# Pricing the other engine's work: a planning model that charges VectorE and GpSimd for steps that overlap

## The chip, the cores and the metric

The kernel runs on one core of one Trainium2 chip. A core has engines that each work through their own queue of instructions in order and wait for each other by semaphores: TensorE (PE, matrix products; PEld is its loading of weights), VectorE (DVE), ScalarE (ACT), GpSimd (POOL) and SyncE (SP), whose queue starts most of the DMAs. What counts is the device time of one execution in microseconds (us): the median of several runs, lower being better. A profiled execution gives a trace; its span is the time from its first to its last instruction.

## What is computed

One layer of a hybrid decoder trunk on 16 learned and 1024 given tokens of 1024 channels. Four token mixers (RWKV-7, gated linear attention, attention over keys selected by an indexer, mLSTM) read one combined input projection; their outputs are gated, summed and projected; then 16 SwiGLU experts follow, of which each token uses two. Cut to the frame:

```python
h = layer_norm(concat(meta, x), ln_in_g, ln_in_b)
p, gates = split(h @ w_in)                  # 1040 tokens; 4 branches, and 4 * 1024 gate channels
y = [rwkv7(p[0]), gla(p[1]), dsa(p[2]), mlstm(p[3])]          # 256 channels each
m = sum(sigmoid(gates[i]) * (y[i] @ w_branch[i]) for i in range(4))
h = layer_norm(alpha * h + m @ w_out, ln1_g, ln1_b)
out = layer_norm(alpha * h + hier_moe(h), ln2_g, ln2_b)       # top group, then top 2 of its 4 experts
```

## The kernel before

Every large product is taken in three passes of a rounded format: a matrix is split into a high part (a cast by ScalarE) and a low part, raw minus high, a subtraction of two operands. The subtractions carry names in the trace: hTl for the normalised input, wl for w_in, fwl for w_branch, yl and zl for the mixers' outputs, wol for w_out, mT0l and s9l for weights of the experts.

**Stages.** In the head (0 to 58 us) `InputNorm` (L368) normalises nine tiles of tokens, lx; VectorE adds, GpSimd multiplies, PE transposes (lp), and ScalarE and VectorE split into hTh and hTl. Then `Products` (L605) runs through w_in in tiles of 128 columns, 2 groups of 24 matmuls into pj each, 148 groups in all. Beside them the mixers run as streams: `rwkv` builds an inverse by forward substitution on GpSimd (ft and TT by turns, about 283 to 355 us) and then goes through a recurrence (xp, xc); `dsa` scores keys at the same time (xa and xb are products, rl the rectified result on ScalarE, sc the weighted sum over heads on VectorE), selects and attends; `gla` and `mlstm` follow. `Merge` (L443) multiplies each branch's output (yh, yl; zh, zl) by w_branch into mz, in rows of two halves of six matmuls, 32 rows in all. A row's gate comes from PE directly (fused) or is read back from memory into g; VectorE makes g times mz, and GpSimd or VectorE adds it to the sum h. From 1217 us on w_out, the second normalisation, the routing, and the experts.

**What sets the order.** Nothing in this order is written out by hand. While the program is built, the class `Order` (L30) keeps a clock for each of four engines, `t`, and moves it with every instruction: `before` (L93) finds when the operands are there, `after` (L133) adds the modelled cost of the step. Streams that are ready by PE's clock go first; where PE would wait, `fill` (L60) draws the next piece of projection work. Three places ask the other clocks too. `free` (L197) gives a step to GpSimd if its clock is behind PE's, else to VectorE (every wl); `sooner` (L201) gives it to whichever would be done first (fwl, yl, zl); and the sums h go to GpSimd unless its clock is 0.6 us ahead of PE's (L600). `more` (L2817) draws pieces of w_out while VectorE's clock is behind PE's. The prices before are a fixed part and a part by size:

```python
return 0.068 + n / 960 + (0.061 if op == "scalar_tensor_tensor" and len(ins) > 2 else 0)    # VectorE, us
...
... 0.14 + n * (0.0044 if op == "tensor_scalar" else 0.0021)                                 # GpSimd, us
...
return self.gpsimd if self.t["gpsimd"] < self.t["tensor"] else self.vector                  # free
```

So what the model holds for an engine's time decides which of two engines gets a step, and in what order the streams' steps and the filling work stand in each queue. Once built, the order is fixed.

Of the kernel before, what the change touches and what calls it, by code (L numbers as in the profile page):

```python
# [15 lines left out]
PSUM = bass.MemoryType.PSUM  # L16
# [13 lines left out]
class Order:  # L30
# [10 lines left out]
    def __init__(self, nc):  # L41
        self.nc = nc
        self.t = {e: 0.0 for e in ("tensor", "vector", "scalar", "gpsimd")}
        self.ready = {}

        self.wrote, self.used = {}, {}

        self.last, self.rings, self.prior = {}, {}, {}
        self.table = 1
        self.tiling = 128, 128  # L50
        self.end = 0.0
        self.dma = 0.0
        self.back, self.in_back = None, False

        self.warm = None
        for e in self.t:
            setattr(self, e, Engine(self, e))
        self.sync = Engine(self, "sync")
# [74 lines left out]
    def after(self, eng, op, kw, out, ins, dep):  # L133
        n = out.free_size()
        if "dma" in op:
            start = max(dep, self.t["tensor"])
            if eng == "gpsimd":
                start = self.t[eng] = max(self.t[eng], dep) + 1.03
            end = max(start + 0.6, self.dma) + n * out.shape[0] * 4 / 340e3
            if start < self.t["tensor"] + 1:  # L140
                self.dma = end
            end += 1.8
        else:
            self.acc = kw.get("accum_out") is not None
            end = self.t[eng] = max(self.t[eng], dep) + getattr(self, "cost_" + eng)(op, out, ins, n)
            end += self.OUT[eng]
            if eng != "tensor":
                for a in [out] + ins:
                    self.note(self.used.setdefault((eng, a.tensor.name), []), a, end)
# [5 lines left out]
        if kw.get("accum_out") is not None:  # L155
            a = kw["accum_out"]
            self.note(self.wrote.setdefault(a.tensor.name, []), a, end)
            self.ready[a.tensor.name] = end
        self.end = end


    TURN = 0.092
# [442 lines left out]
class Products:  # L605
# [127 lines left out]
    def run(self, ln, done, es):  # L733
# [21 lines left out]
        yield from self.gated(self.last, self.after)  # L755

    def gated(self, i, after):

        m, q, nc = self.merge, [], self.k.nc
# [45 lines left out]
        while m.G is None:  # L805
            yield False
            ahead()
        self.flush()
        more = after()
        while True:  # L810
            ahead()
# [2276 lines left out]
```

## Time and profile before

| | us |
|---|---|
| median of three runs | 1682.43 |
| lowest and highest | 1677.73, 1683.59 |
| the profiled execution | 1686.26 |
| its span | 1684.5 |
| PE busy in the span | 1587.0 |
| VectorE, ScalarE, GpSimd busy | 1114.9, 755.7, 431.0 |
| mean granted clock of PE | 0.971 of full speed |

The profiled execution is 3.83 us above the median, and 1.76 of it lie outside the span. Almost all instructions are recorded by one helper, so they bear its line, L268, and are told apart by the names of the tiles that they write and read. A busy engine is one that works on an instruction; waits are idle time before an instruction, with what ended it.

### The profile page before, as it was taken

To read this page: it belongs to the slowest core of one execution; us is meant where nothing else is said; L and a number is where in the kernel's file an instruction comes from. 1 tells how busy PE (TensorE), PEld (TensorE's weight loads), DVE (VectorE), ACT (ScalarE), POOL (GpSimd) and SP (SyncE) were. 2 spreads that over 40 slices of the span, in tenths; PEclk is the share of its full clock that TensorE was granted. 3 is DMA by queue.
4 is the path that set the end of the run, shared out by engine and by line. 5 is a ranking of instruction groups with operands and counts; after the bars stand their busy time and mean duration, and the time that the engine had idled before them with its cause. 6 is when DMAs were issued, how large, how long until landed. Compare 5 with 4: busy or idle time off the path is not lost. (4 is left out here: it accounts for less than half of the span.)

```text
span 1684.5 us, 27808 instructions
## 1 busy us (share of the span) xinstructions
PE 1587.0 (94%) x10020; PEld 1336.2 (79%) x10020; DVE 1114.9 (66%) x2534; ACT 755.7 (45%) x1544; POOL 431.0 (26%) x555
## 2 busy tenths in 40 slices
PE   4999999899999999999999999997999989999985
PEld 3999899788887777777887777775788778898962
DVE  8344755754489898884556477748666668776655
ACT  4334444355544455425444433432121157776645
POOL 5222226831111102123211131126800123111021
PEclk9999999999999999999999998998999989999997
DMA  7874445242322323343211252067512379999855
GB/s 245 240 231 133 146 132 146 80 124 78 91 67 78 83 79 104 95 154 108 69 38 32 86 152 63 28 193 251 180 66 101 126 213 265 287 303 279 269 196 201
DMA packets 240429, 244.86 MB, mean 145 GB/s; under 512 B 39018, under 2 KB 204812, under 8 KB 240288
## 3 DMA queue, kind: packets, MB, share of 16 engines
q1 hardware_dynamic: 234400, 222.08, 43.8%
q0 software_dynamic: 5888, 20.97, 4.4%
q8 instruction: 80, 1.31, 0.3%
q14 instruction: 61, 0.50, 0.1%
HBM read 168.98 MB, written 74.02 MB: 144 GB/s over the span
## 5 line engine op out<-in xcount | busy, mean ns | idle before, releaser
L268 PE MATMUL pj<-hTl,wh 128*128 128x512 f32 (+3 forms) x1184 | 435.5, 368 | 1.0 <-DVE hTl L268 1.0
L268 PE MATMUL pj<-hTh,wh 128*128 128x512 f32 (+3 forms) x1184 | 435.2, 368 | 0.0
L268 PE MATMUL pj<-hTh,wl 128*128 128x512 f32 (+3 forms) x1184 | 431.5, 364 | 0.0
L268 PEld LDWEIGHTS pj<-hTh,wh 128*128 128x128 f32 (+1 forms) x1184 | 225.8, 191 | 26.8 <-issue 2.5
L268 PEld LDWEIGHTS pj<-hTl,wh 128*128 128x128 f32 (+1 forms) x1184 | 225.6, 191 | 26.5 <-issue 1.6
L268 POOL TENSOR_TENSOR wl<-wr,wh 128x256 fp32r<-128x256 f32 (+1 forms) x177 | 137.8, 795 | 422.9 <-ACT wh L268 407.0
L268 PEld LDWEIGHTS pj<-hTh,wl 128*128 128x128 f32 (+1 forms) x1184 | 226.0, 191 | 23.7 <-issue 1.6
L268 ACT COPY pe<-pj 128x384 f32<-128x384 f32 (+3 forms) x84 | 37.4, 445 | 121.9 <-PE pj L268 83.7
L268 DVE SCALAR_TENSOR_TENSOR sc<-rl,wi,sc 128x512 f32<-128x512 f32 (+3 forms) x77 | 58.7, 762 | 42.4 <-ACT rl L268 39.3
L268 ACT CAST wh<-wr 128x256 fp32r<-128x256 f32 (+1 forms) x240 | 85.1, 402 | 1.0 <-DMA wr<-in_w_in_dram 0.9
L268 ACT ACTIVATE pe<-pj 128x512 f32<-128x512 f32 x64 | 38.1, 595 | 100.4 <-PE pj L268 74.8
L268 POOL TENSOR_TENSOR h<-h,g 128x512 f32<-128x512 f32 x46 | 64.7, 1420 | 51.9 <-issue 32.2
L268 POOL DMA_INDIRECT xg<-h1d,ix x32 | 33.7, 1054 | 155.4 <-PE py L268 148.7
L268 ACT ACT_TABLE_LOAD x47 | 60.3, 1283 | 6.3 <-DVE qk L268 2.6
L268 PE MATMUL pg<-xT,mT0h 128*128 128x384 f32 x208 | 62.4, 362 | 0.0
L268 POOL TENSOR_TENSOR sc<-sc,band 128x256 f32<-128x256 f32 (+1 forms) x32 | 24.4, 764 | 124.1 <-DVE sc L268 84.8
L268 PE MATMUL pg<-xT,mT0l 128*128 128x192 f32 x208 | 53.8, 259 | 0.0
L268 DVE TENSOR_TENSOR mT0l<-raw,mT0h 128x1024 fp32r<-128x1024 f32 x35 | 42.5, 1219 | 14.5 <-ACT mT0h L268 13.0
L268 ACT COPY PT<-xb 128x512 f32<-128x512 f32 (+3 forms) x56 | 27.4, 490 | 54.9 <-PE xb L268 52.7
L268 PEld LDWEIGHTS po<-v,PT 128*128 128x128 f32 x352 | 46.3, 192 | 5.6 <-ACT PT L268 2.5
L268 DVE TENSOR_TENSOR wl<-wr,wh 128x256 fp32r<-128x256 f32 x63 | 39.9, 653 | 12.9 <-ACT wh L268 12.8
L268 PE MATMUL po<-v,PT 128*128 128x64 f32 x352 | 47.6, 273 | 0.5 <-ACT PT L268 0.4
(645 smaller groups left out, 3769.5 us busy)
## 6 DMA issues: line engine op xcount, KB each, us to landing
wr<-in_w_in_dram SPq DMA_DIRECT2D x59, 512.0 KB
raw<-in_moe_w_gate_dram SPq DMA_DIRECT2D x32, 512.0 KB
raw<-in_moe_w_up_dram SPq DMA_DIRECT2D x32, 512.0 KB
raw<-in_moe_w_down_dram SPq DMA_DIRECT2D x32, 512.0 KB
gtd<-pe SPq DMA_DIRECT2D x52, 256.0 KB
g<-gtd SPq DMA_DIRECT2D x52, 256.0 KB
ys<-ey SPq DMA_DIRECT2D x14, 768.0 KB
ys<-zero SPq DMA_DIRECT2D x8, 960.0 KB
```

Source lines behind the costliest of these rows:

```text
L268: r = f(*args, **kw)
```

## The change

`Order` keeps, for VectorE and for GpSimd, the modelled intervals of their last twelve steps that read two operands of more than 16 elements a row outside PSUM. When such a step is added on one of the two, its price rises by a share of the time for which it overlaps the other engine's intervals: 0.8 of it on VectorE, 0.3 on GpSimd. The clocks that all choices read move with it.

```diff
--- before.py
+++ after.py
@@ -41,6 +41,8 @@
     def __init__(self, nc):
         self.nc = nc
         self.t = {e: 0.0 for e in ("tensor", "vector", "scalar", "gpsimd")}
+        self.two = {"vector": [], "gpsimd": []}
         self.ready = {}
 
         self.wrote, self.used = {}, {}
@@ -142,7 +144,11 @@
             end += 1.8
         else:
             self.acc = kw.get("accum_out") is not None
-            end = self.t[eng] = max(self.t[eng], dep) + getattr(self, "cost_" + eng)(op, out, ins, n)
+            start = max(self.t[eng], dep)
+            c = getattr(self, "cost_" + eng)(op, out, ins, n)
+            if eng in self.two and self.pair(op, ins):
+                c = self.beside(eng, start, c)
+            end = self.t[eng] = start + c
             end += self.OUT[eng]
             if eng != "tensor":
                 for a in [out] + ins:
@@ -157,6 +163,22 @@
             self.note(self.wrote.setdefault(a.tensor.name, []), a, end)
             self.ready[a.tensor.name] = end
         self.end = end
+
+    SHARED = dict(vector=0.8, gpsimd=0.3)
+    def pair(self, op, ins):
+        return sum(a.space != PSUM and a.free_size() > 16 for a in ins) > 1
+    def beside(self, eng, start, c):
+        other = self.two["gpsimd" if eng == "vector" else "vector"]
+        c += self.SHARED[eng] * sum(max(0.0, min(start + c, b) - max(start, a)) for a, b in other)
+        mine = self.two[eng]
+        mine.append((start, start + c))
+        del mine[:-12]
+        return c
     TURN = 0.092
```

No line that computes is different. The built program has the same 8788 instructions on PE and 1524 on ScalarE; VectorE has 2358 in place of 2364, GpSimd 609 in place of 603. Of the 240 wl GpSimd has 181 in place of 177; yl goes from 2 to 4 on GpSimd, zl and s9l from none to 1, fwl from 4 to 3; VectorE adds g to h three times in place of two. Seven of the 32 rows have fused gates in place of six, so that gate results of 256 KB are written and read back 50 times and not 52.

Three places. First VectorE's queue in the head (lx, hTl and wl as above; bst and mv are batch statistics); before:

```order
16 L268 TENSOR_TENSOR lx_121<-lx_121,gb 128x1024
17 L268 TENSOR_TENSOR lx_123<-lx_123,gb 128x1024
18 L268 TENSOR_TENSOR lx_121<-lx_121,gb 128x1024
19 L268 TENSOR_TENSOR wl<-wr,wh 128x256 x2
20 L268 TENSOR_TENSOR lx_123<-lx_123,gb 128x1024
21 L268 TENSOR_TENSOR wl<-wr,wh 128x256 x2
22 L268 BN_STATS bst_166<-lx_129 128x6
23 L268 TENSOR_TENSOR hTl<-lp,hTh 128x4x128 x2
```

and after:

```order
16 L290 TENSOR_TENSOR lx_121<-lx_121,gb 128x1024
17 L290 TENSOR_TENSOR lx_123<-lx_123,gb 128x1024
18 L290 TENSOR_TENSOR lx_121<-lx_121,gb 128x1024
19 L290 TENSOR_TENSOR wl<-wr,wh 128x256 x4
20 L290 BN_STATS bst_166<-lx_129 128x6
21 L290 TENSOR_TENSOR lx_123<-lx_123,gb 128x1024
22 L290 TENSOR_TENSOR hTl<-lp,hTh 128x4x128
23 L290 BN_STATS bst_166<-lx_129 128x6
```

Four wl stand together now ahead of the next tile's lx addition, and the batch statistics are further ahead.

Next GpSimd's queue towards the end of the forward substitution (ft and TT, which shrink by a column at each step), which ends before ARz is cleared for the recurrence; before:

```order
143 L268 TENSOR_TENSOR TT<-TT,ft 104x33x7
144 L268 TENSOR_TENSOR ft<-Ms,TT 104x204
145 L268 TENSOR_TENSOR TT<-TT,ft 104x34x6
146 L268 TENSOR_TENSOR wl<-wr,wh 128x256
147 L268 TENSOR_TENSOR ft<-Ms,TT 104x175
148 L268 TENSOR_TENSOR TT<-TT,ft 104x35x5
```

and after, some steps earlier:

```order
127 L290 AFFINE_SELECT sc<-sc 128x128
128 L290 TENSOR_TENSOR ft<-Ms,TT 104x351
129 L290 TENSOR_TENSOR TT<-TT,ft 104x27x13
130 L290 TENSOR_TENSOR wl<-wr,wh 128x256
131 L290 TENSOR_TENSOR ft<-Ms,TT 104x336
```

The wl of the first listing is gone from the last fifteen steps; one stands earlier, after the step of 351 columns.

Last VectorE's queue where the merge stretch's first w_out pieces are split; before:

```order
1326 L268 TENSOR_TENSOR wol<-raw,woh 128x1024 x3
1327 L268 TENSOR_TENSOR yl<-fr,yh 128x2x256
1328 L268 SCALAR_TENSOR_TENSOR g<-g,mz 128x512 x2
1329 L268 TENSOR_TENSOR fwl<-fw,fwh 128x256
1330 L268 SCALAR_TENSOR_TENSOR g<-g,mz 128x512 x2
1331 L268 TENSOR_TENSOR fwl<-fw,fwh 128x256
1332 L268 SCALAR_TENSOR_TENSOR g<-g,mz 128x512
1333 L268 TENSOR_TENSOR yl<-fr,yh 128x2x256
1334 L268 SCALAR_TENSOR_TENSOR g<-g,mz 128x512
```

and after:

```order
1325 L290 TENSOR_TENSOR wol<-raw,woh 128x1024 x3
1326 L290 TENSOR_TENSOR yl<-fr,yh 128x2x256
1327 L290 SCALAR_TENSOR_TENSOR g<-g,mz 128x512 x2
1328 L290 TENSOR_TENSOR fwl<-fw,fwh 128x256 x3
1329 L290 TENSOR_TENSOR yl<-fr,yh 128x2x256
1330 L290 TENSOR_TENSOR wol<-raw,woh 128x1024
1331 L290 TENSOR_TENSOR fwl<-fw,fwh 128x256
1332 L290 TENSOR_TENSOR yl<-fr,yh 128x2x256
1333 L290 SCALAR_TENSOR_TENSOR g<-g,mz 128x512
1334 L290 TENSOR_TENSOR h_9861<-h_9861,g 128x512
1335 L290 SCALAR_TENSOR_TENSOR g<-g,mz 128x512
1336 L290 TENSOR_TENSOR zl<-fr,zh 128x2x256
```

The block of three wol is the same; behind it the next fwl, wol and yl stand ahead of the following g, and zl, which came after the seventh wol before, comes between.

## Rows read from the trace of the kernel before

**Rows 1.** The page: its span, and busy time of each engine with share and instructions.

```profile
span 1684.5 us, 27808 instructions
PE 1587.0 (94%) x10020; PEld 1336.2 (79%) x10020; DVE 1114.9 (66%) x2534; ACT 755.7 (45%) x1544; POOL 431.0 (26%) x555
```

**Rows 2.** Stages: length; busy us of PE, PEld, DVE, ACT, POOL; PE clock; DMA; GB/s.

```profile
0.00:58.00 58.00, 33.36 (x188) 29.95 (x189) 46.31 (x83) 29.06 (x55) 27.15 (x27) 0.94 0.68 226
...
283.00:361.00 78.00, 70.03 (x396) 65.14 (x395) 51.80 (x59) 35.68 (x79) 61.20 (x71) 0.93 0.38 103
361.00:612.00 251.00, 250.11 (x2224) 207.47 (x2222) 176.49 (x526) 123.50 (x294) 39.32 (x64) 1.00 0.30 81
612.00:1099.00 487.00, 482.37 (x2744) 382.34 (x2742) 335.45 (x883) 206.55 (x441) 102.08 (x160) 0.98 0.29 85
1099.00:1217.00 118.00, 102.14 (x416) 79.73 (x414) 77.62 (x103) 26.16 (x50) 66.66 (x55) 0.96 0.69 218
1217.00:1400.00 183.00, 173.69 (x1026) 149.93 (x1025) 123.18 (x356) 56.83 (x96) 24.16 (x29) 0.95 0.42 134
```

**Rows 3.** What PE waited for in 0:58: us, times, longest.

```profile
PE lp L268 <- DVE lx L268: 20.7, 4, 16.6
```

**Rows 4.** What PE waited for in 283:361.

```profile
PE xb L268 <- ACT rl L268: 3.6, 3, 1.2
PE xp L268 <- POOL ARz L268: 2.5, 1, 2.5
PE xa L268 <- ACT rl L268: 1.8, 3, 1.2
```

**Rows 5.** What PE waited for in 361:1099, the largest.

```profile
PE x L268 <- DVE e L268: 1.8, 1, 1.8
```

**Rows 6.** What PE waited for in 1099:1217.

```profile
PE mz L268 <- DVE fwl L268: 6.6, 5, 1.9
PE mz L268 <- DVE g L268: 6.4, 5, 1.5
PE mz L268 <- POOL fwl L268: 2.9, 1, 2.9
```

**Rows 7.** DVE in order of time, the additions on lx: start, length, idle before.

```profile
32.30 3.41 DVE L268 TENSOR_TENSOR lx<-lx,gb 128x1024 f32<-128x1024 f32 x1
...
36.83 2.20 DVE L268 TENSOR_TENSOR lx<-lx,gb 128x1024 f32<-128x1024 f32 x1
...
44.11 1.21 DVE L268 TENSOR_TENSOR lx<-lx,gb 128x1024 f32<-128x1024 f32 x1
...
53.28 1.22 DVE L268 TENSOR_TENSOR lx<-lx,gb 128x1024 f32<-128x1024 f32 x1
```

**Rows 8.** POOL in the same stretch.

```profile
29.87 11.38 POOL L268 TENSOR_TENSOR lx<-lx,gb 128x1024 f32<-128x1024 f32 x4 [4.62 <-ACT lx L268]
```

**Rows 9.** DVE in 283:361 by form, min/median/max ns: subtractions wl and score steps.

```profile
L268 DVE TENSOR_TENSOR wl<-wr,wh x14: 572/1106/1261, 292.0 to 347.1; 128x256 fp32r<-128x256 f32 x14
...
L268 DVE SCALAR_TENSOR_TENSOR sc<-rl,wi,sc x35: 351/850/1452, 291.2 to 351.6; 128x512 f32<-128x512 f32 x21, 128x128 f32<-128x128 f32 x7, 128x256 f32<-128x256 f32 x7
```

**Rows 10.** The same score steps on DVE in 361:612.

```profile
L268 DVE SCALAR_TENSOR_TENSOR sc<-rl,wi,sc x28: 606/751/753, 364.3 to 436.3; 128x512 f32<-128x512 f32 x21, 128x384 f32<-128x384 f32 x7
```

**Rows 11.** DVE, the subtractions wol of the whole run.

```profile
L268 DVE TENSOR_TENSOR wol<-raw,woh x8: 1221/2294/2316, 1133.1 to 1172.4; 128x1024 fp32r<-128x1024 f32 x8
```

**Rows 12.** Two stretches with a low PE clock, same columns as rows 2.

```profile
318.50:325.30 6.80, 5.63 (x20) 5.03 (x19) 6.17 (x8) 2.04 (x7) 5.56 (x6) 0.51 0.37 108
356.00:359.40 3.40, 3.40 (x18) 3.38 (x18) 0.00 (x0) 2.61 (x6) 1.31 (x2) 0.53 0.47 112
```

**Rows 13.** PE in order of time: first of twelve mz, and of two following pj groups.

```profile
1106.11 0.39 PE L268 MATMUL mz<-yh,fwh 128*128 128x512 f32 x1
...
1108.89 0.39 PE L268 MATMUL pj<-hTh,wh 128*128 128x512 f32 x1
...
1114.43 0.40 PE L268 MATMUL pj<-hTh,wh 128*128 128x512 f32 x1
```

## The prediction

> **What bounds the kernel now.** I read the page's busy shares first: TensorE (PE) works 1587.0 of 1684.5 us, VectorE (DVE) 66%, GpSimd (POOL) 26% [rows 1]. So the time is PE's own work plus what PE loses, about 97 us, and a change that only moves instructions can win or lose only there. The busy time by stage says where the loss lies [rows 2]: of 0:58 PE is idle 24.6 us, of 283:361 8.0, of 1099:1217 15.9, of 1217:1400 9.3; between 361 and 1099, 738 us of it, only 5.5. Then I asked in those stages what PE waited for. In the head it is lx, the normalised input, four times [rows 3]. In 283:361 it is rl and ARz: rl is an output of ScalarE whose buffers VectorE frees by summing scores, ARz is GpSimd's to clear, behind the forward substitution [rows 4]. In 361:1099 the longest wait is 1.8 us [rows 5]. In 1099:1217, where the last gated products are summed, it is fwl and g, on VectorE but for one fwl on GpSimd, 15.9 us together [rows 6]. These are the stages where VectorE and GpSimd work side by side.
>
> They do disturb each other. In the head three equal 128x1024 additions on VectorE took 3.41, 2.20 and 1.21 us [rows 7]; the slow ones lie under GpSimd's four products, 11.38 us without a gap [rows 8]. Among the scores a 128x256 wl subtraction has a median of 1.11 us and a fastest of 0.57, and a score step goes up to 1.45 [rows 9]; after GpSimd's long run the slowest of the same steps is 0.75 [rows 10]. Of eight wol subtractions the fastest took 1.22 us and the median 2.29 [rows 11].
>
> **What the change does.** No arithmetic and no wait is written differently. The model's price of a two-operand step rises by 0.8 (VectorE) or 0.3 (GpSimd) of its overlap with such steps on the other engine, so on VectorE by at most 0.8 of its own length. By the model's formula a wl subtraction of 0.335 us may become 0.60, a wol one of 1.135 may become 2.04; the rows have 1.11 and 2.29. The sign is right and wol's size nearly, wl's is half. What follows is only a new order: some subtractions change engine (GpSimd gets four more wl of 177, two yl, one zl, one s9l; VectorE one fwl, one h), and PE's streams are handed out at other places. What moves costs the same few microseconds of engines that are not the bound; it counts only where PE waits. By stages:
>
> Head (0:58). VectorE does four wl before the third tile's lx addition where it did two, so that addition comes two wl later, 2 x 0.5 = about 1 us, and what PE does behind it about 2.5 us later with the hTl steps that slipped too. This is not lost for good: PE then waits for lx anyhow. Replaying VectorE's queue in its new order with the durations of these rows, the batch statistics of later tiles come earlier, and the last tile's addition is issued at 51.6 us in place of 53.28 [rows 7], with seven more small products of PE done before it. The first matmuls' delay is inside the 16.6 us wait that ends the longest of the four [rows 3]. I take 1.3 us of gain from the 1.7; the bounds are 0.8 lost (2.5 late, 1.7 regained) and 1.7 won.
>
> Scores beside the substitution (283:361). Three wl stood on GpSimd in front of ARz, now one, and the order gives PE 67.2 groups of 24 projection matmuls before the recurrence's first product in place of 65.9. The first of 24 starts at 1108.89 and the next group's at 1114.43, so a group of 512 columns is 5.54 us [rows 13] and 1.3 of the narrower ones of this stage some 6.5. Against the 2.5 us wait for ARz [rows 4] that is ample: it goes, and with it the stretch at 356.0:359.4 in which the granted clock was 0.53, that is 1.2 GHz, right behind that wait [rows 12]: half of 3.4 us, 1.7. Of the rl waits, 5.4 us together [rows 4], the five long ones are of about 1.2; with one wl less among the score steps of 306 to 320 at 1.11 us [rows 9] and another now and then moved, I take 1.7 off. Together 5.9. From below: if both clock and rl stay, 2.5; from above all of 5.4 + 2.5 + 1.7 and the half of 318.5:325.3 (3.4) [rows 12], 13.
>
> Recurrence to the last stream (361:1099). Between the recurrence's first and last product PE has 26.8 groups in place of 29.2, so 2.4 x 5.54 = 13.3 us less to do while it waits for that chain; from the selection of keys to the end of the last mixer 1.5 groups and two halves of 6 matmuls less, 11 us (twelve mz matmuls go from 1106.11 to 1108.89, so a half is 1.39) [rows 13]. The work is not lost, it stands later. It costs only where the cover was thin. PE was idle 0.9 us of 251 in 361:612 and 4.6 of 487 after it [rows 2], so the trace does not show how much of the cover was spare. Bounds: 0, and the whole 13.3. I take 1.0, near the low end: no wait of this stage is above 1.8 [rows 5], and 2.4 of 29.2 groups is a twelfth of the cover.
>
> The merge stretch (1099:1217). From 1108.89 PE had two groups and 27 rows of two halves, 11.1 + 27 x 2.78 = 86 us, and took until 1217: 22 lost, of which the waits are 15.9 [rows 6] and the clock some 4.7 (0.96 of 118) [rows 2]. After the change the last stream ends about 19 us of PE's work sooner, so that six groups instead of three and 29 rows remain, and three pairs of groups stand between rows: there the staging of y and z and three wol run beside projections instead of beside rows that each need a g and an fwl. But 22 rows still follow the last pair, the three wol still stand in one block before the first g, and each row still asks VectorE for two g, one fwl and the h that GpSimd does beside it. Counting the waits of the new order by hand with these durations gives the same 16 us within what I can tell. I take 0, with 5 either way.
>
> Experts and end (1217 on). The order is the same but for one s9l, at 1400 us, that goes from VectorE (1.22 us as the fastest wol of the same shape [rows 11]) to GpSimd, where a gather queues behind it; 0, with 1 either way.
>
> The sum is -1.3 - 5.9 + 1.0 + 0 + 0 = -6.2, on the profiled execution's 1686.26 us: 1680.1. That execution was 3.83 above the median of 1682.43, so I say 1676.5 for the median.
>
> The Trainium skill, on its page "SBUF — State Buffer", section "Who interferes with whom", says that a VectorE step with two inputs in SBUF and a GpSimd step that reads SBUF hold the port they share in turn, each for its whole length, and that the one that comes second stands still. The 3.41 us beside 1.21 agrees: 2.2 us more is most of a GpSimd product of 2.85 (11.38 / 4) and more than the 0.8 x 1.21 = 0.97 that the change would charge. By that rule each of the eight subtractions that the new order moves to GpSimd (four wl, two yl, one zl, one s9l) stands once in the way of a VectorE step, at 1.11 - 0.57 = 0.54 us each [rows 9]; were all of it on the path, the sum would be -6.2 + 4.3 = -1.9 by the rule.
>
> **The rivals.** *The merge stretch opens* (against: 22 rows in a line at the end). If the three pairs of groups take up the wol block and the staging, only the tail's waits stay. Half of the 15.9 us and one clock dip of 3.4 us at half speed (1.7) would go: 9.6 more, about 1667.
>
> *The recurrence runs bare* (slower). Its steps are a chain PE, VectorE, ScalarE, PE; with 13.3 us less between its ends PE would stand whenever a step's own chain is longer than the work put between. It decides from the point where the spare of the cover, not seen in the trace, is under 13.3 us. If none of it was spare: +13.3, and one dip as at 318.5:325.3 (half of 6.8 us, 3.4) [rows 12]: 1676.5 - 1.0 + 16.7 = about 1692. For it: 0.9 us of idle time says the old cover was just used up or more. Against: no wait there is even 1 us.
>
> *The order hardly matters* (it doesn't do what it says). The charge meets at most half of what a wl loses, few subtractions change engine, and the waits of the merge and score stages come back beside other work. Then only the ARz wait goes, or is paid for elsewhere: 1680 to 1685, say 1682. The rule of the Trainium skill's page "SBUF — State Buffer", section "Who interferes with whom", speaks for this rival: if the later step stands still for the rest of the other engine's, a charge by the share of its own length misses the price.
>
> **How the numbers follow.** Forecast 1676.5: 0.40. The merge stretch opens, 1667: 0.20. The order hardly matters, 1682: 0.25. The recurrence runs bare, 1692: 0.15. About 0.5% (8.4 us) is what a measurement of this kernel can tell from no change, so faster means under 1674.0 and slower over 1690.8. Faster: most of the merge rival and two fifths of the forecast, whose own spread is some 6 us: 0.18 + 0.16 = 0.34. Slower: 0.10 of the recurrence rival and a few hundredths of the others: 0.13. Same: 0.53. The range reaches from a merge stretch that opens by more than half (1664) to a recurrence with almost no spare (1691).
>
> **What would show it.** Right: no wait for ARz before the recurrence, and no low clock behind it; waits for rl near 3.7 us; PE idle 361:1099 near 6.5 us; in the merge stretch fwl and g again near 16 us; the last lx some 1.7 us sooner. Wrong: PE waiting for the recurrence's steps (xc, xp) or the last mixer's by more than 5 us, or a merge stretch whose waits halve or double, or a clock below 0.97 over the span.

## The result: the changed order is slower by about 10 us

| | before | changed |
|---|---|---|
| median of eight runs, us | 1679.1 | 1688.81 |
| lowest and highest, us | 1675.39, 1683.59 | 1686.5, 1695.72 |
| the profiled execution, its span, us | 1686.26, 1684.5 | 1690.72, 1688.9 |
| mean granted clock of PE | 0.971 | 0.972 |

The ratio is 1.0064, 95% interval 1.0045 to 1.0082: slower by 9.7 us, by more than the 0.5% of the prediction. The forecast was 1676.5, a gain; the time lies in the range (1664 to 1691), on the other side of no change. The changed kernel measured again later gave 1.0065 (1.0043 to 1.0087).

The two profiled spans differ by 4.4 us and not by 9.7: the execution profiled before lay 7.2 us above its median of eight runs, that of after 1.9. So single stages are compared below with further traces of either order too.

First the busy times on the page of the changed kernel, as [rows 1]:

```profile
PE 1580.8 (94%) x10020; PEld 1331.6 (79%) x10020; DVE 1118.9 (66%) x2528; ACT 755.6 (45%) x1544; POOL 436.1 (26%) x561
```

PE is idle 108.1 us, where it was 97.5. The stages, with the columns of [rows 2]:

```profile
0.00:58.00 58.00, 31.82 (x187) 29.11 (x188) 48.64 (x82) 28.40 (x54) 28.41 (x27) 0.97 0.71 234
283.00:361.00 78.00, 69.37 (x400) 64.31 (x399) 48.26 (x58) 34.25 (x79) 59.76 (x69) 0.97 0.34 90
361.00:612.00 251.00, 246.41 (x2195) 204.96 (x2194) 179.85 (x534) 124.83 (x296) 35.86 (x60) 0.99 0.31 82
612.00:1099.00 487.00, 480.22 (x2767) 381.49 (x2766) 338.82 (x879) 207.51 (x443) 105.25 (x165) 1.00 0.32 93
1099.00:1217.00 118.00, 102.68 (x422) 80.73 (x421) 72.52 (x95) 26.32 (x51) 72.38 (x60) 0.92 0.59 180
```

Length minus PE's busy time gives the idle time. In 283:361 it is 8.6 us, where it was 8.0: in the score stage, from which the forecast took most of its gain, no idle time went, and only the clock is somewhat better, 0.97 for 0.93. From 361 to 1099 it is 4.6 + 6.8 = 11.4, where it was 5.5. The merge stretch has 15.3 for 15.9. What PE waited for at the recurrence's start, 283:375 (us, times, longest), to be held against [rows 4]:

```profile
PE xa L290 <- ACT rl L290: 4.9, 6, 1.3
PE xp L290 <- ACT UV L290: 2.3, 1, 2.3
PE xp L290 <- issue: 1.5, 1, 1.5
PE pj L290 <- ACT pe L290: 1.3, 1, 1.3
PE xb L290 <- ACT rl L290: 0.2, 1, 0.2
```

The wait for ARz is gone, as forecast. In its place stand three waits of 5.1 us together, for steps of ScalarE (the one put down to "issue" too, below). How long each of the three is differs from trace to trace (in e1, the same kernel again, 0.9 + 2.5 + 2.2). And the waits for rl are 5.1 us for 5.4, not 3.7.

**Where they come from.** SyncE's queue before, from 339 us, in order of time (start, length of the start):

```profile
339.03 0.34 SPq L268 DMA_DIRECT2D pD<-pe  x1
...
342.92 0.34 SPq L268 DMA_DIRECT2D pD<-pe  x1
348.19 0.32 SPq L268 DMA_DIRECT2D td<-TT  x1
```

and after:

```profile
329.52 0.32 SPq L290 DMA_DIRECT2D pD<-pe  x1
346.31 0.34 SPq L290 DMA_DIRECT2D td<-TT  x1
346.70 0.58 SPq L290 DMA_DIRECT2D BKg<-bkd  x1
347.38 2.06 SPq L290 DMA_DIRECT2D pD<-pe  x1
...
355.59 0.54 SPq L290 DMA_DIRECT2D pD<-pe  x1
...
357.73 0.40 SPq L290 DMA_DIRECT2D pD<-pe  x1
```

pe is the copy that ScalarE takes of a finished projection group; it has three buffers, and a buffer is free when its store to memory (pD) has landed. td is the store of the substitution's result TT, ready at 346.3. Before, td stood behind the pe stores. Now it stands ahead of three of them, and SyncE starts nothing from 329.84 to 346.31. ScalarE behind it (idle time and what ended it in brackets):

```profile
353.09 0.48 ACT L290 COPY pe<-pj 128x384 f32<-128x384 f32 x1 [4.29 <-DMA pD<-pe]
...
357.69 0.39 ACT L290 COPY pe<-pj 128x272 f32<-128x272 f32 x1 [3.19 <-DMA pD<-pe]
358.10 0.58 ACT L290 COPY UV<-xp 40x512 f32<-40x512 f32 x1
...
361.66 1.04 ACT L290 CAST qs<-qi 128x1024 fp32r<-128x1024 f32 x1 [2.55 <-DMA qi<-pC]
362.73 0.69 ACT L290 ACTIVATE KB<-xp,half 104x512 f32<-104x512 f32 x1
```

The stores leave at 347.38 and, behind loads that need td's landing, at 355.59, so the copies wait until 353.09 and 357.69, and UV, the recurrence's first step on ScalarE, stands behind the second. KB stands behind qs, whose input is one more load of the same queue; PE's product xp starts at 363.51, when KB's 0.69 us are over, so its "issue" is KB. The granted clock in the window right behind the wait for UV (it ended at 358.73) and at two later places (columns of [rows 2]):

```profile
359.20:362.60 3.40, 2.79 (x10) 2.28 (x8) 0.00 (x0) 0.94 (x1) 1.17 (x2) 0.50 1.01 257
458.20:461.60 3.40, 3.19 (x29) 2.63 (x30) 3.00 (x12) 1.67 (x4) 0.00 (x0) 0.50 0.00 1
1403.70:1410.50 6.80, 5.55 (x13) 3.77 (x14) 6.18 (x27) 2.63 (x4) 0.00 (x0) 0.50 0.41 122
```

0.50 is 1.2 GHz. A wait of 1.6 to 2.3 us (at the third place two, of 2.2 and 1.9) is followed there by 3.4 us at half the clock, at the third place by 6.8, and half of PE's busy time in it is lost on top of the wait.

The second place, 458.2, is in the recurrence. VectorE, before and then changed:

```profile
466.95 1.20 DVE L268 TENSOR_SCALAR_CACHE_REDUCE junka<-sc 128x1024 bf16<-128x1024 f32 x1
```

```profile
456.80 1.21 DVE L290 TENSOR_SCALAR_CACHE_REDUCE junka<-sc 128x1024 bf16<-128x1024 f32 x1
...
457.94 0.41 DVE L290 TENSOR_SCALAR UV<-xc 40x256 f32<-40x256 f32 x1
```

UV, a step of the recurrence, stands behind the counting steps of the key selection (junka), which reach VectorE 10 us earlier in the recurrence than before. PE's wait for it, 1.6 us, is in every trace with the changed order at this place (also e1, e3, e5, e10, e13 and e17), whatever SyncE's queue does there; the old order has 0.5. PE's waits of 361:1099, as [rows 5]:

```profile
PE xp L290 <- issue: 1.7, 2, 1.5
PE xc L290 <- DVE UV L290: 1.6, 1, 1.6
PE x L290 <- DVE hall L290: 1.5, 3, 0.6
PE po L290 <- ACT PT L290: 1.5, 1, 1.5
PE x L290 <- DVE e L290: 1.2, 1, 1.2
PE pj L290 <- ACT pe L290: 1.2, 1, 1.2
```

No long wait, but five of 1.2 to 1.6 us. In the merge stretch, as [rows 6]:

```profile
PE mz L290 <- DVE g L290: 10.8, 5, 6.0
PE mz L290 <- POOL fwl L290: 2.9, 1, 2.9
```

Five waits for VectorE's fwl have gone, and one of 6.0 us for g has come: behind the block of wol, as long as what it replaces.

**The experts.** One instruction moved there, s9l. VectorE and then GpSimd at 1396 us:

```profile
1396.80 2.37 DVE L290 TENSOR_SCALAR fs<-sf 128x16 f32<-128x16 f32 x1
```

```profile
1396.15 2.98 POOL L290 TENSOR_TENSOR s9l<-raw,s9h 128x1024 fp32r<-128x1024 f32 x1 [1.52 <-ACT s9h L290]
```

fs took 0.16 us before. In the changed kernel with s9l alone back on VectorE:

```profile
1399.91 0.17 DVE L290 TENSOR_SCALAR fs<-sf 128x16 f32<-128x16 f32 x1
```

So one subtraction given to GpSimd cost a step of VectorE 2.2 us, and that step reads one operand, of 16 elements: the change, which charges steps with two operands of more than 16, prices it at nothing. The Trainium skill, page "SBUF — State Buffer", section "Who interferes with whom", says that a `tensor_scalar` can take the shared port pair as well, and that the later of the two stands still; these two rows agree: fs starts 0.65 us after s9l and ends with it, at 1399.17 and 1399.13.

### The profile page after: what moved, and what is told of

Same layout as the page of the kernel before. It is cut to its first block, busy times and chain, and to the rows that moved or that the text cites. A ratio compares the mean times of both kernels' runs of the same rounds, so it can differ in the third digit from the quotient of the medians.

```text
span 1688.9 us, 27785 instructions
## 1 busy us (share of the span) xinstructions
PE 1580.8 (94%) x10020; PEld 1331.6 (79%) x10020; DVE 1118.9 (66%) x2528; ACT 755.6 (45%) x1544; POOL 436.1 (26%) x561
## 5 line engine op out<-in xcount | busy, mean ns | idle before, releaser
L290 POOL TENSOR_TENSOR wl<-wr,wh 128x256 fp32r<-128x256 f32 (+1 forms) x181 | 141.9, 800 | 437.1 <-ACT wh L290 418.8
L290 ACT CAST wh<-wr 128x256 fp32r<-128x256 f32 (+1 forms) x240 | 85.8, 402 | 1.1 <-DMA wr<-in_w_in_dram 1.0
L290 ACT CAST mT0h<-raw 128x1024 fp32r<-128x1024 f32 x36 | 37.6, 1051 | 23.2 <-DMA raw<-in_moe_w_up_dram 10.1
```

The costliest lines, as they stand in the source:

```text
L290: r = f(*args, **kw)
```

## Experiments

All were timed in five rounds beside the kernel before on the same chip. The stages meant by "charge only where" are cut by the model's own clock of PE (`self.t["tensor"]`), which runs behind the real one; outside the cut the price is the old one. The order behind a cut still shifts somewhat, since the plan goes on from where the cut left it.

To compare traces beyond one profile's luck, PE's whole loss was added up in each: its idle time, and half of the time in which it worked at the lower clock, up to the last product. The first column is how long SyncE stood for TT (its wait list, 283:370).

| kernel | SyncE for TT, us | PE idle + clock loss, us | ratio (95%) |
|---|---|---|---|
| before | 4.8 | 87.6 + 39.3 = 126.9 | 1 |
| e18 before, td by GpSimd | 4.9 | 89.5 + 32.2 = 121.7 | 1.0011 (0.9990 to 1.0032) |
| e2 charge in the head | 4.9 | 92.7 + 26.4 = 119.1 | 0.9970 (0.9953 to 0.9986) |
| e4 charge behind the recurrence | 5.2 | 85.8 + 28.8 = 114.6 | 0.9983 (0.9962 to 1.0005) |
| e11 charge in the tail | 4.8 | 91.4 + 29.0 = 120.4 | 1.0013 (0.9997 to 1.0030) |
| e8 charge in all but the scores | 4.8 | 89.1 + 28.2 = 117.3 | 0.9996 (0.9976 to 1.0016) |
| e14 e8 with s9l back | 4.8 | 88.1 + 21.6 = 109.7 | 0.9982 (0.9962 to 1.0002) |
| e15 double charge | 4.1 | 87.1 + 25.7 = 112.8 | 0.9937 (0.9916 to 0.9959) |
| changed | 16.4 | 98.3 + 34.5 = 132.8 | 1.0064 (1.0045 to 1.0082) |
| e1 changed again | 17.5 | 97.0 + 35.9 = 132.9 | 1.0065 (1.0043 to 1.0087) |
| e13 changed, s9l back | 17.5 | 98.8 + 33.5 = 132.3 | 1.0058 (1.0037 to 1.0078) |
| e17 changed, td by GpSimd | 17.5 | 100.1 + 32.9 = 133.0 | 1.0066 (1.0043 to 1.0089) |
| e3 charge in the scores | 16.3 | 99.5 + 25.0 = 124.5 | 1.0041 (1.0020 to 1.0061) |
| e7 charge on GpSimd alone | 14.6 | 91.9 + 34.2 = 126.1 | 1.0025 (1.0007 to 1.0042) |
| e12 charge on VectorE alone | 16.5 | 99.3 + 29.0 = 128.3 | 1.0064 (1.0044 to 1.0084) |
| e16 half the charge | 14.6 | 108.2 + 31.5 = 139.7 | 1.0143 (1.0112 to 1.0175) |
| e9 before, three wl to VectorE | 15.3 | 95.0 + 24.2 = 119.2 | 1.0007 (0.9993 to 1.0022) |
| e10 changed, four wl to GpSimd | 3.7 | 98.8 + 36.4 = 135.2 | 1.0052 (1.0032 to 1.0072) |
| e5 changed, pe stores by ScalarE | 17.5 | 106.8 + 32.6 = 139.4 | 1.0101 (1.0076 to 1.0126) |
| e6 before, pe stores by ScalarE | 9.8 | 93.1 + 26.6 = 119.7 | 1.0010 (0.9992 to 1.0029) |

Three things stand in it. The traces of the changed order (changed, e1, e13, e17) have 97 to 100 us of idle time, where the seven traces whose order from the scores to the recurrence is the old one (before, e18, e2, e4, e11, e8, e14) have 86 to 93. Every kernel in which SyncE stands over 14 us for TT has a higher ratio than every one with 4.1 to 5.2, but for e9 (and e7 can't be told from e11 by its interval); e10 (3.7) is slow too, below. And the clock column varies from trace to trace of nearly one order (39.3 against 32.2, before and e18), so a single profile doesn't tell it well.

The same loss by stage, idle time + clock, shows where the orders differ:

| traces | 283:361, us | 361:612, us |
|---|---|---|
| the seven with the old order there | 11.7 to 12.6 | 0.9 to 1.4 |
| the four of the changed order | 10.1 to 11.5 | 6.7 to 9.0 |
| e3 charge in the scores | 12.2 | 9.6 |

So the score stage gained about 1 us, and 6 to 8 us were lost behind it, in the recurrence.

**Which stage (e1 to e4, e8, e11).** The edit, with another bound for each:

```diff
-            if eng in self.two and self.pair(op, ins):
+            if eng in self.two and self.pair(op, ins) and self.t["tensor"] < 50:
```

e2 is the line above; e3 has `50 <= t < 315`, e4 `575 <= t < 940`, e8 `not 50 <= t < 575`, e11 `t >= 940`. A charge between 315 and 575 alone moves no instruction. e1 is the changed kernel again.

> The changed kernel once more, for a second trace and a closer ratio. All theories: 1.006 of before, some 10 us more. Theory A (the recurrence runs bare): PE's idle time between the recurrence's first xp and its last product is again near 6.8 us, where the first trace of before has 0.8, and the waits for pe, UV and ARz at its start are there again. Theory B (the loss is in the tail of the program, 1217 us on, where the first trace had 4.5 us more of idle time): 30 us of idle time from there on, as in the first trace. What is only in one of the two traces was chance.

> The charge is made only while the model's PE clock is under 50 us, so only the head has the new order; every later row is as before. The prediction's step gave -1.3 us. Theory A: +0 to +1.5 us (the first trace of the changed kernel had 1.6 us more of idle time by the head's end, and 1.3 less lost to the clock). Theory C, that the head makes the loss: +5 us or more.

> The charge is made only while the model's PE clock is between 50 and 315 us, which takes in the scores beside the forward substitution; the head is as before, and what follows is ordered at the old prices, from engine clocks that the charge moved. Recurrence after 67.1 projection groups and over in 26.9, as in the changed kernel. Theory A: +6 to +10 us. Theory B (the order of the merge and later stages, made at the new prices): within 3 us of before. Theory C: within 3 us.

> The charge is made only while the model's PE clock is between 575 and 940 us, after the recurrence and before the merge stretch; up to there all is as before. The last stream ends one group and half a row sooner than before, and eight rows of the merge stand before the last projection in place of five. Theory A: within 3 us of before. Theory B: +4 us or more, from the merge stretch.

> The charge is made everywhere but while the model's PE clock is between 50 and 575 us: the new head, the old order from the scores to the end of the recurrence, new prices after it. If the parts add up (head 0.997, after the recurrence 0.998): ratio 0.995, 9 us under before, and some 18 under the changed kernel. If one of the two was chance: 0.997 to 1.0.

> The charge is made only while the model's PE clock is at or over 940 us: merge stretch, w_out and experts; all before is as before. In the traces with new prices there (the changed kernel twice, and all but the scores) PE waits 2.8 us for hdh at the expert product of s6h and 2.2 us at that of mT0h, where the traces with old prices have 1.2 and nothing. If that is the order of the experts (one s9l on GpSimd): the same two waits here, 2 to 3 us, ratio 1.000 to 1.002. The prediction had 0, with 1 either way: neither wait, ratio within 0.1% of 1.

The head's charge alone gains 0.3%, more than any forecast had; in its trace the clock of 41:50 is 0.81 where it was 0.62. The charge behind the recurrence and that of the tail can't be told from no change. The charge in the score stage loses 0.41%, 6.9 us, and the kernel with everything but that has 0.9996. So the loss comes in with the order of the score stage and what follows from it; by e3's trace it stands in 361:612 and not among the scores. The parts don't add up (-0.30 + 0.41 - 0.17 + 0.13 = 0.07%, measured 0.64%), and e8 missed its 0.995: an order is not a sum of orders.

**Is it SyncE's queue (e5, e6, e9, e10, e17, e18)?** In e5 and e6 the pe stores around the recurrence's start go out by ScalarE, in the changed kernel and in the one before:

```diff
-                nc.sync.dma_start(dst[:, o - META:o - META + m] if gate else dst[:, o:o + m], e[r:r + q, 0:m])
+                by = nc.scalar if 305 < nc.t["tensor"] < 340 else nc.sync
+                by.dma_start(dst[:, o - META:o - META + m] if gate else dst[:, o:o + m], e[r:r + q, 0:m])
```

> The changed kernel; seven stores of projection results (pD<-pe, those issued while the model's PE clock is between 305 and 340 us) are started by ScalarE's queue, behind the copy that fills the buffer, in place of SyncE's. PE, VectorE and GpSimd have word for word the changed kernel's order. Theory D: in the changed kernel the store of the forward substitution's result (td<-TT), for which SyncE waits until 346.3 us, stands ahead of four such stores and not of one; the three pe buffers stay full, ScalarE's next copy waits until 353.1, and UV, KB and PE's recurrence behind it. Then PE's idle time from the recurrence's first product to its last (6.2 to 7.4 us in three traces) falls to 2.5 us or less, the wait for pe before it goes too, and the time comes 4 to 6 us under the changed kernel's: ratio to before 1.002 to 1.004. Theory A in its first form (too little work between the steps of the chain, whatever the queue): the idle time stays above 5 us, ratio 1.006.

> The same for the kernel before, as a control: what the move of the stores alone does. Theory D: nothing much (the trace of before has no wait for pe there): within 2 us of before; ScalarE spends some tenths of a us on each store. Theory A: the same.

e5 gave 1.0101 (1.0076 to 1.0126), e6 1.0010 (0.9992 to 1.0029). ScalarE in e5:

```profile
350.22 0.37 ACTq L290 DMA_DIRECT2D pD<-pe  x1
350.69 0.60 ACT L290 ACTIVATE rl<-xb 128x512 f32<-128x512 f32 x1 [14.21 <-DMA BKg<-bkd]
```

The store was put off until a load of SyncE's queue, BKg, had landed, and ScalarE with it, 14.21 us; PE stood 13.2 for rl. This is of the program and not of the chip: as built, ScalarE waits before such a store for the last transfer that raises the same semaphore, here BKg, in e6 td (4.55 us). The waits at UV and KB were gone, but the edit made a worse one: it decides nothing.

e9 does it from the other side: in the kernel before, three wl of the score stage run on VectorE in place of GpSimd, and the model isn't told. e10 gives four wl from VectorE to GpSimd in the changed kernel (`305 < t < 321`, to "gpsimd").

```diff
-                nc.free().tensor_sub(lo[:, t, 0:n], raw[:, t, 0:n], hi[:, t, 0:n].bitcast(F32))
+                by = nc.free().name
+                aps = lo[:, t, 0:n], raw[:, t, 0:n], hi[:, t, 0:n].bitcast(F32)
+                w = nc.before(by, "tensor_sub", aps, {})
+                getattr(nc.nc, "vector" if 250 < nc.t["tensor"] < 318 and by == "gpsimd" else by).tensor_sub(*aps)
+                nc.after(by, "tensor_sub", {}, *w)
```

> The kernel before, with the three wl subtractions that GpSimd does among the last part of the forward substitution done by VectorE; the model is not told, so PE, ScalarE and the rest keep word for word the order of before. Only SyncE's queue differs by it: td (the store of the substitution's result) now stands ahead of three stores of projection results, as in the changed kernel. Theory D: PE's idle time between the recurrence's first and last product rises from 0.7 us (four traces of that order) to 4 us or more, with waits for pe or UV, and the ratio is 1.002 to 1.004. The prediction's step (less work on GpSimd lets ARz come sooner): the 2.5 us wait goes and the ratio is 0.997 to 1.0.

> The changed kernel, with four wl of the score stage done by GpSimd in place of VectorE, the model not told. PE's order is the changed kernel's; SyncE's queue has td behind the three stores again. Theory D: the idle time between the recurrence's first and last product falls from 6.2 to 7.4 us to 3 us or less, although GpSimd has 3 to 4 us more to do, and the ratio from 1.0065 to 1.002 to 1.005. The rival (the recurrence has too little work between its steps, or GpSimd's load is what counts): idle time 6 us or more, ratio 1.0065 or above.

In e9 the substitution ends earlier, SyncE's queue is built with td ahead of the pe stores (so that queue isn't settled by the model, which was not told), and the same wait of ScalarE is there, with PE behind it:

```profile
350.58 0.48 ACT L268 COPY pe<-pj 128x384 f32<-128x384 f32 x1 [4.22 <-DMA pD<-pe]
```

```profile
351.40 0.47 PE L268 MATMUL xb<-kis,qs 128*128 128x256 f32 x1 [3.99 <-ACT rl L268]
```

But the wait for ARz goes with it, and the time is 1.0007. So the rows show link by link how td's place makes this wait of PE. With the ARz wait (2.5 us) taken off against it, the sum is 1 us, by the interval at most 4, less than theory D had forecast. e10 takes SyncE's wait away (3.7 us) and lengthens GpSimd's chain instead:

```profile
358.13 1.07 PE L290 MATMUL xp<-ident,BKg 128*104 128x128 f32 x4 [5.00 <-DMA TS<-td]
```

PE now waits 5.0 us for the substitution's result, and the time is 1.0052, hardly below the changed kernel's. Held against each other, 361:612 of e9 and then of e10 (columns of [rows 2]):

```profile
361.00:612.00 251.00, 248.98 (x2209) 206.00 (x2208) 177.41 (x525) 123.77 (x296) 40.21 (x64) 1.00 0.31 82
361.00:612.00 251.00, 247.12 (x2193) 205.89 (x2192) 177.32 (x528) 121.17 (x289) 36.05 (x59) 0.98 0.30 79
```

e9, with td ahead but PE's old order, is idle 2.0 us there and never at the lower clock. e10, with td late but PE's changed order, is idle 3.9 us, and 4.4 more go by the clock. Theory D had 4 us or more for e9's recurrence and 3 or less for e10's: both missed. In these traces the loss of the recurrence goes with the order of PE's streams, and not with SyncE's queue.

e17 moves the one store: GpSimd, which makes TT, starts td, and the orders of PE, ScalarE and VectorE stay as in the changed kernel. e18 is the same in the kernel before.

```diff
-            nc.sync.dma_start(td, TT)
+            w = nc.before("sync", "dma_start", (td, TT), {})
+            nc.nc.gpsimd.dma_start(td, TT)
+            nc.after("sync", "dma_start", {}, *w)
```

> The changed kernel with one instruction given to another queue: the store td of the substitution's result is started by GpSimd, which has made it, in place of SyncE; the orders of TensorE, ScalarE and VectorE are those of the changed kernel. Theory (the store td, ahead of the pe stores in SyncE's queue, makes the waits at the recurrence's start): SyncE no longer stands 16 us for TT, the first of the pe stores goes out near 334 us, ScalarE's pe copy at 353.1 no longer waits for it, TensorE's wait for pe (1.3 us) goes, and with it most of those for UV (2.3) and behind qs (1.5); 3 to 5 us of waits and perhaps a dip of the clock (1.7), against up to 1 us by which GpSimd's start of the store is later: ratio to before 1.002 to 1.005. Rival (the result's landing bounds the start, whatever the queue does): the waits take another name, at TS or ARz, and the ratio stays at 1.006 to 1.008.

> The control: the same one store given to GpSimd in the kernel before, where it stood behind the three pe stores. Theory: nothing to free, so no gain; the store starts as before or up to 1 us later, which the wait for ARz (2.5 us) would show: ratio 0.999 to 1.002. Rival (a start by GpSimd is itself better or worse): outside of that in either direction.

1.0066, as the rival had it. SyncE and then ScalarE in e17:

```profile
346.09 0.59 SPq L290 DMA_DIRECT2D BKg<-bkd  x1
```

```profile
353.70 0.48 ACT L290 COPY pe<-pj 128x384 f32<-128x384 f32 x1 [6.11 <-DMA pD<-pe]
```

The load BKg, next in the queue, now waits for TT as td did (17.5 us by the wait list; TT's last step ends at 346.06), with the pe stores behind it again. So the instruction at the head of the queue is exchangeable; the wait of the copies comes of something that needs TT standing ahead of stores that don't. A queue without that and with the changed kernel's order of PE and GpSimd was not made, so its worth there stays unmeasured. e18 (1.0011) is within its forecast: the start by GpSimd itself costs nothing that can be told.

**Which price, and how much of it (e7, e12, e15, e16).**

```diff
-    SHARED = dict(vector=0.8, gpsimd=0.3)
+    SHARED = dict(vector=1.6, gpsimd=0.6)
```

is e15; e16 has 0.4 and 0.15, e7 0.0 and 0.3, e12 0.8 and 0.0.

> Only GpSimd's steps are charged (0.3), VectorE's are not (0.0). The head is then as before, and the recurrence begins after 67.0 projection groups as in the changed kernel, so it is GpSimd's price, by which the forward substitution looks longer, that moves it. Theory D: SyncE's queue has td ahead of the stores again; 6 us of idle time in the recurrence and a ratio of 1.003 to 1.006. If it is VectorE's price that costs: within 0.2% of before.

> Only VectorE's steps are charged (0.8), GpSimd's are not. The recurrence begins after 65.9 groups as before, but 24.8 groups lie between its first and last step in place of 26.8 (29.2 before is counted to its very end in the same way); td stands ahead of three stores. Theory D: idle time of 3 us or more at the recurrence's start, ratio 1.001 to 1.004. If only the later start of the recurrence costs: as the head alone, 0.997.

> Charges of 1.6 and 0.6 in place of 0.8 and 0.3, nearer to what the rows show a VectorE step to lose (1.1 for 0.5). If the time follows from how true the price is: better than the changed kernel, ratio under 1.004. If any new order costs about as much, since the order of before is a good one among many and each new one puts a few steps where something waits: 1.002 to 1.008, not to be told from the changed kernel. If it is GpSimd's load beside the substitution: the recurrence after 69.8 groups in place of 67.2, ratio above 1.0065.

> Charges of 0.4 and 0.15. If the loss grows with the charge: 1.002 to 1.004. If any new order costs about as much: 1.002 to 1.008 as before; the last stream ends at 139.9 groups here, sooner than in every other order, so more cover is missing in the mixers (46.1 groups from the recurrence's start to the end of the last mixer's groups in place of 49.9 for the changed kernel counted alike), and if cover counts it is the slowest of all.

Charging GpSimd alone (e7, 1.0025) comes in just under its forecast, with 4.1 us of idle time in the recurrence where 6 had been expected. Charging VectorE alone (e12) gives 1.0064, as slow as both together, over its forecast, and its recurrence is covered: 361:612 loses 1.0 us, with 24.8 groups where the changed kernel has 26.8 and with SyncE standing 16.5 us. Before the recurrence PE waits 5.4 us for rl there, behind a pe copy as in e9, and from 1217 us on the loss is 46.0 us, for 40.4 before; neither was tried by itself. Neither that queue nor the count of groups alone says whether the recurrence waits.

No charge 1, half 1.0143, whole 1.0064, double 0.9937: the time does not follow the price, though the double charge, which comes nearest to what the rows show a wl to lose, is the fastest. It beats both kernels (1669.77 us, where the kernel before had 1680.56 on that chip). Two stages of it, columns of [rows 2]:

```profile
283.00:361.00 78.00, 73.62 (x447) 69.75 (x446) 55.59 (x66) 37.31 (x86) 58.35 (x67) 1.00 0.36 101
...
1099.00:1217.00 118.00, 107.00 (x442) 85.01 (x441) 75.76 (x109) 29.27 (x54) 70.64 (x57) 0.93 0.62 192
```

and its SyncE queue:

```profile
342.28 6.78 SPq L290 DMA_DIRECT2D pD<-pe  x3
353.23 0.33 SPq L290 DMA_DIRECT2D td<-TT  x1
```

PE is idle 4.4 us in the score stage for 8.0, with no stretch at the lower clock, and 11.0 in the merge stretch for 15.9. The pe stores stand ahead of td, the recurrence starts after 69.8 projection groups (67.2 changed, 65.9 before), and neither ARz nor UV is waited for. In the half charge SyncE stands 14.6 us for td, which leaves at 350.55, and then PE waits:

```profile
367.25 1.00 PE L290 MATMUL xp<-ARz,BKg 128*104 128x160 f32 x4 [4.55 <-issue]
```

and in its merge stretch a single wait of 7.4 us for zl. That its loss is more than the changed kernel's shows at several such places (3.5 us more idle time in the head, 13.4 us of loss in 361:612, the merge), none of which was tried by itself. Its expectation had said that it would be the slowest of all if cover counts, and it is; e12 above speaks against cover as the one cause.

**The moved subtraction of the experts (e13, e14).** s9l goes back to VectorE, in the changed kernel and in e8; the model isn't told.

```diff
+            getattr(nc.nc, "vector" if by == "gpsimd" and lo.tensor.name.startswith("s9l") else by).tensor_sub(*aps)
```

> The changed kernel with one subtraction of 240 KB less for GpSimd: the s9l of the experts that the new prices gave to GpSimd is done by VectorE again, the model not told; every other instruction of every queue is the same. In the traces with that s9l on GpSimd a 128x16 step of VectorE beside it (fs<-sf) takes 2.37 us where it takes 0.17 without, and PE waits 2.2 us more for hdh. Theory E (that step stands still until GpSimd's is over, and the experts' chain with it): fs takes 0.2 us, the wait for hdh at mT0h goes, the time falls 2 to 4 us, ratio 1.004 to 1.0055. The prediction's step (0, with 1 either way): 1.006 to 1.007.

> New prices everywhere but from 50 to 575 us of the model's PE clock, with that one s9l on VectorE. If the parts add up (0.9996 for it with s9l on GpSimd, less the 2 to 4 us): ratio 0.997 to 0.9985, faster than both kernels. If the s9l is worth nothing: 0.9996.

1.0058 for 1.0065, 0.9982 for 0.9996: both some 1 to 2 us better, and neither can be told from no difference by its interval. Theory E's 1.004 to 1.0055 for e13 was missed narrowly, e14 is within its forecast. The row of fs above shows what happens at the step. Of what PE waits for behind it, one wait is shorter. PE in the changed kernel and then in e13:

```profile
1402.32 0.47 PE L290 MATMUL py<-mT0h,hdh 128*96 128x512 f32 x1 [2.22 <-ACT hdh L290]
```

```profile
1404.41 0.47 PE L290 MATMUL py<-mT0h,hdh 128*96 128x512 f32 x1 [1.34 <-ACT hdh L290]
```

The wait for hdh falls by 0.9 us; that for hdl, 1.93 us in both, stays, and the clock behind both is 0.66 over 10 us in either (1.00 before). So s9l is the smaller part of what this place lost.

## Why the prediction was wrong

**What bounds the kernel** was right: the change is won and lost in PE's losses, and its idle time rose by 10.6 us from profile to profile. Two terms of the sum failed, the scores and the recurrence. (Less 3.83, the sum gives 1676.2, where the prediction says 1676.5; nothing hangs on it.)

**Head, -1.3.** Right in sign, by luck as far as the traces show. The head's order alone gives 0.9970, 2 to 8 us of gain, but not in the head: in 0:58 e2 loses 26.0 us idle and 1.7 by the clock, where the kernel before lost 24.6 and 3.0. Where it gains was not located. The step itself was wrong: the last lx addition did not come sooner. Its start is 54.54 us, where it was 53.28, and the head's idle time rose by 1.5.

**Scores, -5.9: the first step that failed.** The stage gained about 1 us (10.1 to 11.5 us of loss for 11.7 to 12.6). The step's first half held: one wl in place of three ahead of ARz, and the wait for ARz went (2.5). Its end did not. The prediction followed GpSimd, VectorE and PE and took SyncE's queue as it was. In the changed program what needs TT stands ahead of the pe stores, SyncE stood 16.4 us for 4.8, three buffers of pe were full, and ScalarE's copies passed the wait on to PE: 2.3 + 1.5 + 1.3 us in place of 2.5, and 3.4 us at half the clock in place of the 3.4 that were to go. The trace of before had both halves of it: SyncE's rows, and three pe buffers. The saving of 1.7 on rl was not there either (5.1 us for 5.4). e9 has this queue without the loss (1.0007), so in these runs the queue accounts for the gain that didn't come, and not for the loss.

**Recurrence to the last stream, +1.0: the second step that failed, and the one in which the loss stands.** In 361:612 alone the loss by idle time and clock went from 0.9 to 1.4 us to 6.7 to 9.0. From profile to profile idle time rose by 5.9 us in 361:1099, within the bounds of 0 to 13.3. The prediction took the low end because no wait there was above 1.8 us and the cover shrank by a twelfth only; but a stage with almost no waits shows no spare, and steps that came a little late were waited for. Its sign of being wrong came true: PE's waits at the recurrence's xp and xc are 2.3 + 1.7 + 1.6 = 5.6 us, over the 5 that it had named. The rival of a bare recurrence (1692) had the right side and nearly the time. Its mechanism isn't shown: the waits that the rows explain are for links that stood behind other work of ScalarE and VectorE, and e12, with less cover still, has 1.0 us. Of the 5.9, 1.5 are the late start (KB's product) and 1.6 the key selection at UV; the others are mostly waits for pe (1.2), PT (1.5) and hall (1.5 in three). Which move of the order brings each of these about stays open. The price of a wait was also taken too low: the one at 458 us for UV has 3.4 us at half the clock behind it, so its 1.6 us cost 3.3.

**Merge, 0 with 5 either way.** Right: 15.3 for 15.9 us, with the clock 21.6 for 20.6, and one wait of 6.0 in place of five for fwl. The rival that it opens did not come true here; it did in e15 (11.0).

**Experts, 0 with 1 either way.** Too low. From 1217 us on, idle time and clock cost 38.2 to 40.6 us in the traces with the old prices there (before, e18, e2, e4) and 41.3 to 47.7 in seven with the new ones (changed, e1, e13, e17, e8, e11, e14), some 4 us more; the timed run of the tail alone, e11, has 2 us more and can't be told from none. s9l lay on the path, for 0.9 us of a wait by the trace and 1 to 2 us by e13 and e14. The rest of what that place lost (1.34 + 1.93 us of waits for 1.46 before, and a granted clock of 0.66 over 10 us, in e13 too) comes from the shifted order, and no run here separates it. The Trainium skill (page "SBUF — State Buffer", section "Who interferes with whom") says that the later step stands still until the first is over. The prediction worked out from it that each subtraction moved to GpSimd stands once in the way of a VectorE step; that holds at this one, with 2.2 us at the step and not the 0.54 that the wl rows had given.

**The rival that the order hardly matters** had part of the truth: the charge's size decides little about the steps that it prices, and the sum of the moves came out by other places than those that the charge is about.

## What to carry to other kernels

When a planner's price changes, don't take a chain that hardly waits for one with cover to spare: here steps of the key selection that came 10 us earlier made it wait 1.6 us. Look at the in-order queue that starts the DMAs as well as at the engines: for each instruction that moves past others, ask what it waits for and which buffers are freed only behind it. A truer price need not give a better order (half and whole charge are truer than none and slower): in these traces the time hangs on a few places that the model doesn't see. Try several sizes of it and keep the one that measures best. A new wait of PE is to be priced with the clock behind it.

## What was not expected of the hardware

- A step of VectorE with one operand of 128x16 took 2.37 us beside a GpSimd subtraction of 2.98, and 0.16 to 0.17 without it.
- The lower clock behind a short wait does not always come. In the changed kernel's two traces the same wait for pe at 437 us (1.21 and 1.25) is followed by full clock in 440.1:443.5 of the first and by 0.51 in 440.3:443.7 of the second.

Open are three things: which moves of the order make the recurrence wait, what SyncE's wait is worth in the changed kernel, and why the half charge loses 24 us.
